# A mixture-of-experts layer whose expert passes 8 to 10 are added back by matmuls instead of by a store and a gather

## The chip, the cores and the metric

One core of one Trainium2 chip runs the whole layer. The metric is the time of one execution on the device, in microseconds (us). Before the change it is 538.73 us, the median of three runs (537.30 to 542.03).

## What is computed

One decoder layer over 512 tokens of width 1024: a projection, four mLSTM heads and eight sliding-window attention heads side by side, an output projection, a layer norm, a two-level mixture of experts (each token picks the best of 4 groups, then the best 2 of the 8 experts in it), and a second layer norm. The change lies in the mixture of experts:

```python
g_idx = jnp.argmax(g_logits, axis=-1)
e_in = jnp.take_along_axis(e_logits, g_idx[:, None, None], axis=1)[:, 0]
top_v, top_i = lax.top_k(e_in, TOP_K_INNER)                      # 2 of 8
top_w = jax.nn.softmax(top_v, axis=-1) * g_p[:, None]
...
for e in range(N_EXPERTS):                                       # 32 experts
    h = jax.nn.silu(xt @ w_exp_gate[e]) * (xt @ w_exp_up[e])     # 1024 -> 256
    out = out + combine[:, e:e + 1] * (h @ w_exp_down[e])        # 256 -> 1024
x = layer_norm(ALPHA * x + out, ln2_w, ln2_b)
```

## The kernel before, in words

The first half of the kernel (projection, heads, first norm, routing) ends at about 269 us and is not touched. What follows are the expert passes.

**Passes.** The 1024 assignments (512 tokens, two experts each) are laid into 13 passes of 128 rows, `ORDER = "BBBABABACBBCC"`. A pass of kind A or B holds two experts, one of kind C four. The six experts of passes 0 to 2 are fixed, the others are ordered by how many tokens chose them, fullest first. Every expert has 3 MB of weights; they stream in through a ring of 16 buffers of 1 MB, in the order of the passes, at most eight transfers at a time. SP's queue issues them, and an issue waits until TensorE has read what the buffer held.

**One pass.** `taken(p)` brings the token rows of two passes, transposed, into `xs`. For most passes it does this by one-hot matmuls (`pairs_x`, 64 matmuls of 128x256; `hots` makes the one-hot tiles `ohr` on VectorE). For the pairs in `GATHER` (4 and 5, 6 and 7) it takes rows that GpSimd's indirect DMA fetched from the copy `xd` of the activations in DRAM (`fetch`, tile `xg`) and turns them by 16 transposes (`pairs_g`). `pass_gu` multiplies by the gate and up weights in four steps; before the last step it turns the hidden rows of the pass before (`dn_t`: two transposes into `ph`, then VectorE copies them to `ht`). `pair_h` makes the hidden rows on ScalarE and VectorE (`hid`). `pass_dn` multiplies the hidden rows of the pass before by the down weights.

**Adding back.** `y_store` scales the result (ScalarE) and GpSimd's queue stores it to the DRAM buffer `yd`. `y_gather` fetches for each chunk of 128 tokens and each of its two experts the row of `yd` (tile `yg`, eight gathers of 512 KB), and VectorE adds it to the sum `x1`. Passes 0 to 10 (`KEPT` = 11) go this way, and `EARLY` puts the eight gathers at the start of pass 11, behind the down product of pass 10. An assignment to pass 11 or 12 reads a row of zeros that the kernel wrote behind the others. Pass 11 goes back by `add_back`: 16 matmuls of 128x512 with a one-hot tile `oh2` (tiles `cb`, two PSUM banks in turn), each pair followed by a VectorE add to `x1`. The rows of pass 12 are handled in the last section.

**Order.** TensorE's order is written out by hand; in the last section (from `p = NP - 1`) that of VectorE, ScalarE and GpSimd too. Every engine executes its own list in order. Tiles `y`, `yg`, `xg`, `xs`, `ohr`, `yh`, `yl`, `oh2` share one pool of 16 buffers ("mix"), so a new tile waits until the last reader of its buffer is done.

## Time and profile before

| | |
|---|---|
| median of 3 runs | 538.73 us |
| the profiled execution | 538.57 us, its span 536.7 us |
| mean granted TensorE clock | 0.929 of full speed |
| TensorE matmul busy | 472.7 us, 88% of the span |
| VectorE, ScalarE, GpSimd busy | 260.8, 163.1, 152.4 us |
| moved by DMA | 139.43 MB, mean 260 GB/s |

The span is the time from the first to the last instruction in the profile; 1.9 us of the execution lie around it. In the rows below L1007 is the matmul of the picks (`pick`), L1062 the transposes of fetched rows, L1094 the gate/up products, L1115 and L1117 the transposes and the copy in `dn_t`, L1125 the down product, L1143 the store to `yd`, L1150 and L1152 the gathers and their adds, L1171 and L1172 the matmuls and adds of `add_back`. The profile counts each gate/up and down matmul twice.

### The profile page before, as it was taken

How to read it: one execution, taken by the hardware profiler on the slowest of the kernel's cores; microseconds unless marked ns; L12 is line 12 of the kernel's file. 1: busy time of each engine (PE TensorE's matmuls, PEld its weight loads, DVE VectorE, ACT ScalarE, POOL GpSimd, SP SyncE). 2: the span in 40 equal slices, each digit the busy share in tenths (PEclk: the TensorE clock that was granted, in tenths of full speed). 3: DMA queues.
4: the chain of work that ended last, by engine and by line, in shares of the span. 5: the costliest groups of instructions: out<-in, count | busy, mean ns of one | idle time of the engine just before them, and what ended most of it. 6: DMA issues, size and time to landing. Idle time of an engine off the chain costs nothing. (4 is left out here: it accounts for less than half of the span.)

```text
span 536.7 us, 8111 instructions
## 1 busy us (share of the span) xinstructions
PE 472.7 (88%) x2904; PEld 315.7 (59%) x2904; DVE 260.8 (49%) x589; ACT 163.1 (30%) x352; POOL 152.4 (28%) x178
## 2 busy tenths in 40 slices
PE   6999899999999999977899999999687996628990
PEld 5999688879899987766735633426112631324420
DVE  3453678884278675688973110303000300144883
ACT  3553545786444322414311111211110111000430
POOL 5479903422120111645821100000000001311451
PEclk9899979999999999999699999999977998757896
DMA  8624212220983539197559999999999999999504
GB/s 231 205 80 122 76 40 78 79 79 8 349 312 96 183 116 280 43 357 255 216 187 394 406 419 406 403 422 395 379 421 422 419 419 422 422 416 423 234 19 159
DMA packets 44907, 139.43 MB, mean 260 GB/s; under 512 B 6386, under 2 KB 17674, under 8 KB 41024
## 3 DMA queue, kind: packets, MB, share of 16 engines
q1 hardware_dynamic: 40944, 126.05, 62.7%
q0 software_dynamic: 3920, 12.84, 6.3%
q8 instruction: 24, 0.39, 0.3%
q14 instruction: 19, 0.16, 0.1%
HBM read 128.68 MB, written 10.49 MB: 259 GB/s over the span
## 5 line engine op out<-in xcount | busy, mean ns | idle before, releaser
L1094 PE MATMUL pg<-we,xs 128*32 128x512 f32 (+1 forms) x608 | 114.0, 645 | 16.1 <-DMA we<-in_w_exp_up 16.1
L1094 PEld LDWEIGHTS pg<-we,xs 128*32 128x32 f32 (+1 forms) x608 | 29.0, 127 | 86.9 <-issue 74.0
L245 PE MATMUL pj<-wh,xh 128*128 128x256 f32 (+1 forms) x224 | 63.8, 287 | 0.6 <-ACT wh L190 0.6
L246 PE MATMUL pj<-wh,xl 128*128 128x256 f32 (+1 forms) x224 | 62.8, 282 | 0.3 <-DVE xl L191 0.3
L1007 PE MATMUL xp<-ohr,x1h 128*128 128x256 f32 (+1 forms) x160 | 45.0, 314 | 18.3 <-ACT xs L1015 8.8
L250 PE MATMUL pj<-wl,xh 128*128 128x256 f32 x192 | 52.5, 279 | 0.0
L1143 POOL DMA_DIRECT2D yd<-y x11 | 6.1, 557 | 158.1 <-ACT y L1142 158.1
L1117 DVE COPY ht<-ph 128x256 f32<-128x256 f32 x13 | 5.5, 423 | 91.9 <-PE ph L1115 91.9
L1125 PE MATMUL yo<-we,ht 128*32 128x512 f32 (+1 forms) x304 | 47.4, 595 | 2.4 <-DVE ht L1117 1.8
L1007 PEld LDWEIGHTS xp<-ohr,x1h 128*128 128x128 f32 x160 | 34.6, 217 | 22.9 <-ACT xs L1015 8.9
L1007 PE MATMUL xp<-ohr,x1l 128*128 128x256 f32 (+1 forms) x160 | 44.1, 309 | 0.0
L245 PEld LDWEIGHTS pj<-wh,xh 128*128 128x128 f32 x224 | 42.4, 189 | 0.9 <-ACT wh L190 0.8
L246 PEld LDWEIGHTS pj<-wh,xl 128*128 128x128 f32 x224 | 42.4, 189 | 0.6 <-DVE xl L191 0.6
L1107 ACT ACTIVATE hid<-pg 128x256 f32<-128x256 f32 x13 | 5.0, 385 | 122.8 <-PE pg L1094 122.8
L250 PEld LDWEIGHTS pj<-wl,xh 128*128 128x128 f32 x192 | 35.6, 188 | 0.0
L1007 PEld LDWEIGHTS xp<-ohr,x1l 128*128 128x128 f32 x160 | 35.0, 219 | 0.0
L191 DVE TENSOR_TENSOR wl<-wraw,wh 128x1024 fp32r<-128x1024 f32 x14 | 21.2, 1528 | 23.0 <-ACT wh L190 22.9
L1125 PEld LDWEIGHTS yo<-we,ht 128*32 128x32 f32 (+1 forms) x304 | 14.4, 119 | 29.2 <-issue 24.4
L190 ACT ACTIVATE wh<-wraw 128x1024 fp32r<-128x1024 f32 (+2 forms) x23 | 23.2, 1021 | 12.3 <-DMA wraw<-in_w_in 3.5
L194 PE MATMUL pj<-xh,wh 128*128 128x512 f32 x64 | 26.7, 417 | 0.0
L196 PE MATMUL pj<-xl,wh 128*128 128x512 f32 x64 | 26.5, 414 | 0.0
L195 PE MATMUL pj<-xh,wl 128*128 128x512 f32 x64 | 26.3, 411 | 0.0
(363 smaller groups left out, 908.2 us busy)
## 6 DMA issues: line engine op xcount, KB each, us to landing
we<-in_w_exp_gate SPq DMA_DIRECT2D x64, 512.0 KB, 11.8
we<-in_w_exp_up SPq DMA_DIRECT2D x64, 512.0 KB, 12.2
we<-in_w_exp_down SPq DMA_DIRECT2D x30, 1024.0 KB, 13.5
wraw<-in_w_in SPq DMA_DIRECT2D x20, 512.0 KB, 3.7
yd<-y POOLq DMA_DIRECT2D x11, 512.0 KB, 7.6
xc<-in_x SPq DMA_DIRECT2D x4, 512.0 KB, 10.0
wo<-in_w_out SPq DMA_DIRECT2D x8, 256.0 KB, 5.0
wo<-in_w_out SPq DMA_DIRECT2D x4, 512.0 KB, 3.6
```

What stands on the lines that cost most here:

```text
L190: A.activation(hi, src, AF.Copy)
L191: eng.tensor_tensor(lo, src, hi, op=OP.subtract)
L194: TE.matmul(o, lh, rh, start=start, stop=False)
L195: TE.matmul(o, ll, rh, start=False, stop=False)
L196: TE.matmul(o, lh, rl, start=False, stop=stop)
L245: TE.matmul(o, xh[j // 2][:, j % 2, cs], ws[i][j][0], start=j == 0, stop=False)
L246: TE.matmul(o, xl[j // 2][:, j % 2, cs], ws[i][j][0], start=False, stop=False)
L250: TE.matmul(o, xh[k // 2][:, k % 2, cs], ws[i][k][1], start=False, stop=k == 7)
L1007: TE.matmul(p_[:, j2, 0:P * n], w[c][:, 2 * g + j2], o[:, c, 0:P * n], start=c == 0 and s == 0 and j2 == 0, stop=c == NCH - 1 and s == 1 a ...
L1094: TE.matmul(pg[s:s + n], xs[k // 4][:, k % 4, P * b + s:P * b + s + n], ws[e][k // 4][:, :, k % 4], start=k == 0, stop=k == 7)
L1125: TE.matmul(py[u][s:s + n], ht[:, j, s:s + n], wt[e][2][j][:, 512 * u:512 * u + 512], start=j == 0, stop=j == 1)
L1143: G.dma_start(yd[p * P:(p + 1) * P], y)
```

## The change

`KEPT` becomes 8 and `GATHER` becomes empty. So:

- all token rows come by one-hot matmuls; the four fetches from `xd` in the loop and their 32 transposes are gone;
- passes 0 to 7 are stored to `yd`, 8 to 10 go back by `add_back`, behind the down product of each, inside passes 9, 10 and 11;
- the eight gathers come in two groups of four: behind the store of pass 7 (in pass 8), and behind the add-back of pass 8 (in pass 9);
- the row of zeros is gone: each `yg` tile is set to zero by GpSimd, and the gather has a bound, so that rows beyond `yd` are left as they are;
- `EARLY` is gone: pass 10's down product stands behind the picks of pass 12 again, as in the other passes.

```diff
-GATHER = (4, 6)
-EARLY = (NP - 2,)
-KEPT = NP - 2
+GATHER = ()
+KEPT = 8
...
-    yd = DR.tile([KEPT * P + 1, DM], F32, name="yd")
+    yd = DR.tile([KEPT * P, DM], F32, name="yd")
...
-    def y_gather():
-        for c in range(NCH):
+    def y_gather(cs):
+        for c in cs:
             for k in range(2):
                 t = slot("yg")[:, :DM]
+                G.memset(t, 0.0)
                 G.indirect_dma_start(out=t, out_offset=None, in_=yd[:, :],
-                                     in_offset=bass.IndirectOffsetOnAxis(ap=yrow[:, 2 * c + k:2 * c + k + 1], axis=0))
+                                     in_offset=bass.IndirectOffsetOnAxis(ap=yrow[:, 2 * c + k:2 * c + k + 1], axis=0),
+                                     bounds_check=KEPT * P - 1, oob_is_err=False)
                 V.tensor_add(x1[c], x1[c], t)
...
-        V.tensor_scalar(yrow, col, float(KEPT * P), None, op0=OP.min)
+        V.tensor_copy(yrow, col)
...
-            early = p in EARLY
-            if early:
-                y_store(pass_dn(dn_t(prev), p - 1), p - 1)
-                y_gather()
             hts = []
-            pg = pg2 if p == 2 else pass_gu(xs, p % 2, p, (lambda: hts.append(dn_t(prev))) if prev and not early else None)
-            if hts:
+            pg = pg2 if p == 2 else pass_gu(xs, p % 2, p, (lambda: hts.append(dn_t(prev))) if prev else None)
+            if prev:
                 ht = hts[0]
...
-            if prev and not early:
-                y_store(pass_dn(ht, p - 1), p - 1)
+            if prev:
+                py = pass_dn(ht, p - 1)
+                if p - 1 < KEPT:
+                    y_store(py, p - 1)
+                else:
+                    y = y_split(py, cws[:, p - 1:p], *y_slots())
+                    add_back(back_hot(slot("oh2", F32R)[:, 0:T], toks(p - 1)), y)
+                if p - KEPT in (0, 1):
+                    y_gather(range(2 * (p - KEPT), 2 * (p - KEPT) + 2))
```

The functions that it now calls in the loop stood in the kernel before and served pass 11 (line numbers of before):

```python
    def y_split(py, cs, yh, yl):                                              # L1131
        for u in range(2):
            us = slice(512 * u, 512 * u + 512)
            A.activation(yh[:, us], py[u], AF.Copy, scale=cs)
            V.scalar_tensor_tensor(yl[:, us], py[u], cs, yh[:, us], op0=OP.mult, op1=OP.subtract)
...
    def add_back(o, y, cs=range(NCH)):
        for c in cs:
            for u in range(2):
                us = slice(512 * u, 512 * u + 512)
                b = bank("cb", tag="pj")
                for i, t in enumerate(y):
                    TE.matmul(b, o[:, c * P:(c + 1) * P], t[:, us], start=i == 0, stop=i == 1)   # L1171
                V.tensor_add(x1[c][:, us], x1[c][:, us], b)                                      # L1172
```

What moves on the engines is shown at three places: VectorE around the gathers, GpSimd's list, and VectorE in the tail. First VectorE's list before, in pass 11 (`ht` and `hid` are those of pass 10's and pass 11's hidden rows, `yg` the gathered rows, `xs` the picked rows for pass 12):

```order
L1117 COPY ht<-ph 128x256
L1152 TENSOR_TENSOR x_2218<-x_2218,yg 128x1024 x2
L1152 TENSOR_TENSOR x_2221<-x_2221,yg 128x1024 x2
L1152 TENSOR_TENSOR x_2224<-x_2224,yg 128x1024 x2
L1152 TENSOR_TENSOR x_2227<-x_2227,yg 128x1024 x2
L1108 TENSOR_TENSOR hid<-hid,pg 128x256
L1013 COPY xs<-xp 128x2x128
```

All eight adds stand together there, ahead of pass 11's hidden rows and of the copy of the picked rows. VectorE's list after the change, from the hidden rows of pass 8 on (the first `ht` below is pass 8's, in the middle of pass 9; the second is pass 9's, in the middle of pass 10):

```order
L1106 TENSOR_TENSOR hid<-hid,pg 128x256
L1152 TENSOR_TENSOR x_2217<-x_2217,yg 128x1024 x2
L1152 TENSOR_TENSOR x_2220<-x_2220,yg 128x1024 x2
L1115 COPY ht<-ph 128x256
...
L1172 TENSOR_TENSOR x_2226<-x_2226,cb 128x512 x2
L1152 TENSOR_TENSOR x_2223<-x_2223,yg 128x1024 x2
L1152 TENSOR_TENSOR x_2226<-x_2226,yg 128x1024
L1115 COPY ht<-ph 128x256
L1152 TENSOR_TENSOR x_2226<-x_2226,yg 128x1024
L1106 TENSOR_TENSOR hid<-hid,pg 128x256
```

Four adds now stand ahead of pass 8's `ht`, and three more, behind the eight adds of pass 8's add-back, ahead of pass 9's `ht`. GpSimd's list after the change from the first store on (before it was a store, two fetches of `xg`, a store, two fetches, nine stores and the eight gathers):

```order
L1141 DMA yd<-y 128x1024 x7
L1148 MEMSET yg 128x1024 x2
L1141 DMA yd<-y 128x1024
L1148 MEMSET yg 128x1024 x2
L1149 DMA yg<-yd,yrow 128x1024 x4
L1148 MEMSET yg 128x1024 x2
L1149 DMA yg<-yd,yrow 128x1024 x2
```

The first four gathers stand behind the eighth store; of the last four the first pair is shown, and the second follows in the same way behind the setting of its tiles. And VectorE's list after the change, in the tail, from the last add of pass 10's add-back to pass 11's `ht` (`ohr` are the one-hot tiles for the rows of pass 12; before, they were made while the picks of pass 12 ran):

```order
L1172 TENSOR_TENSOR x_2226<-x_2226,cb 128x512 x2
L190 TENSOR_TENSOR l2w<-trif,l2w 16x128
L1159 TENSOR_SCALAR oh_4644<-iot,tok_2107 128x256
L1159 TENSOR_SCALAR oh_4644<-iot,tok_2108 128x256
L998 TENSOR_SCALAR ohr<-iot,pcol 128x128
L1000 SCALAR_TENSOR_TENSOR ohr<-iot,pcol,ohr 128x128
...
L1115 COPY ht<-ph 128x256
```

Pass 11's `ht` stands behind the adds of pass 10 and behind eleven small instructions.

## Rows read from the trace of the kernel before

**Rows 1.** The page's part 2: DMA's busy tenths in 40 slices of 13.4 us.

```profile
DMA  8624212220983539197559999999999999999504
```

**Rows 2.** Busy time by stretch: length, PE, PEld, DVE, ACT, POOL, granted clock, DMA share, GB/s.

```profile
405.00:410.00 5.00, 3.10 (x8) 0.77 (x8) 0.00 (x0) 0.00 (x0) 0.00 (x0) 0.54 1.03 421
...
485.00:490.00 5.00, 5.00 (x24) 3.62 (x28) 3.77 (x11) 0.00 (x0) 1.36 (x1) 0.50 1.03 421
490.00:495.00 5.00, 4.48 (x42) 1.34 (x38) 0.42 (x1) 0.00 (x0) 0.00 (x0) 0.93 1.03 423
...
500.00:505.00 5.00, 5.00 (x23) 1.41 (x22) 4.19 (x9) 3.54 (x5) 2.76 (x7) 0.66 0.71 298
```

**Rows 3.** Timeline of TensorE, picks and transposes: start, busy us, line, operation, idle before.

```profile
293.58 0.39 PE L1007 MATMUL xp<-ohr,x1h 128*128 128x256 f32 x1
...
301.08 0.28 PE L1007 MATMUL xp<-ohr,x1l 128*128 128x256 f32 x1
...
315.88 1.16 PE L1062 MATMUL xp<-ident,xg 128*128 128x128 f32 x8
...
318.47 3.65 PE L1125 MATMUL yo<-we,ht 128*64 128x512 f32 x16
```

**Rows 4.** Timeline of TensorE, passes 5, 7, 8 and 10.

```profile
332.96 5.33 PE L1094 MATMUL pg<-we,xs 128*32 128x512 f32 x48
...
340.51 1.16 PE L1062 MATMUL xp<-ident,xg 128*128 128x128 f32 x8
...
357.59 4.47 PE L1094 MATMUL pg<-we,xs 128*32 128x512 f32 x38
...
366.61 0.39 PE L1007 MATMUL xp<-ohr,x1h 128*128 128x256 f32 x1
...
377.97 1.06 PE L1094 MATMUL pg<-we,xs 128*32 128x512 f32 x6
...
397.63 3.62 PE L1125 MATMUL yo<-we,ht 128*32 128x512 f32 x32
...
440.91 3.65 PE L1125 MATMUL yo<-we,ht 128*64 128x512 f32 x16 [0.56 <-ACT y L1142]
```

**Rows 5.** Timeline of TensorE, picks of pass 12 and down product of pass 11.

```profile
474.51 0.48 PE L1007 MATMUL xp<-ohr,x1h 128*128 128x128 f32 x1 [8.79 <-ACT xs L1015]
...
484.73 0.47 PE L1007 MATMUL xp<-ohr,x1h 128*128 128x128 f32 x1 [6.54 <-DVE xs L1013]
...
492.38 3.64 PE L1125 MATMUL yo<-we,ht 128*32 128x512 f32 x32 [0.52 <-DVE ht L1117]
```

**Rows 6.** Timeline of GpSimd: the last store and the first gather.

```profile
445.59 0.53 POOL L1143 DMA_DIRECT2D yd<-y  x1 [4.08 <-ACT y L1142]
454.08 0.98 POOL L1150 DMA_INDIRECT yg<-yd,yrow  x1 [7.97 <-issue]
```

**Rows 7.** Timeline of VectorE, from the first gathered row's add to pass 11's add-back.

```profile
462.72 1.23 DVE L1152 TENSOR_TENSOR x<-x,yg 128x1024 f32<-128x1024 f32 x1 [21.91 <-DMA yg<-yd,yrow]
...
472.70 1.23 DVE L1152 TENSOR_TENSOR x<-x,yg 128x1024 f32<-128x1024 f32 x1 [1.30 <-DMA yg<-yd,yrow]
...
482.78 1.23 DVE L1152 TENSOR_TENSOR x<-x,yg 128x1024 f32<-128x1024 f32 x1 [1.27 <-DMA yg<-yd,yrow]
483.93 0.41 DVE L1108 TENSOR_TENSOR hid<-hid,pg 128x256 f32<-128x256 f32 x1
...
484.59 0.27 DVE L191 TENSOR_TENSOR l2w<-trif,l2w 16x128 fp32r<-16x128 f32 x1
...
488.50 0.42 DVE L1013 COPY xs<-xp 128x256 f32<-128x256 f32 x1
...
497.48 1.36 DVE L1172 TENSOR_TENSOR x<-x,cb 128x512 f32<-128x512 f32 x2
```

**Rows 8.** Groups of instructions on GpSimd: busy us, mean ns of one.

```profile
L389 POOL MEMSET pr<- 128x256 f32 x4 | 1.1, 308 | 0.0
```

**Rows 9.** The DMA issues: count, median us to landing.

```profile
out<-z,row POOLq DMA_INDIRECT x1, 3.3
```

More of the change, by code (lines that the diff above doesn't have):

```diff
@@ L663, in layer_kernel @@
                 need(1)
-    SP.dma_start(yd[KEPT * P:KEPT * P + 1].rearrange("o (k n) -> (o k) n", k=8), warm[0:8])
     identb = C.tile([P, P], BF16, name="identb")
```

## The prediction

> **What bounds the kernel now.** I read the slices first: the DMA engines are full from about 282 us on and empty again at about 503 [rows 1, 2]. This is the weight stream, and one would think that the end is the stream's end. The timelines say otherwise for the last stage. In the picks for pass 12 TensorE stands twice, 8.8 and 6.5 us, for ScalarE's and VectorE's copies of picked rows [rows 5]. VectorE at that time adds gathered rows, one when each gather lands, from 462.72 to 484.0; the hidden rows and the copy that TensorE needs are queued behind the eighth add [rows 7]. From 484.7 TensorE runs on into the down product of pass 11 at 492.38 [rows 5], and from there to the end, 44.3 us later (536.7), stands the tail that the change leaves as it is. The last weights land by about 503 [rows 2]; what needs them is the down product of pass 12, near the end. So the end is set by when the down product of pass 11 can start: now by the gathers, 492.38. I work out that moment for the changed kernel. Before pass 8 the stream does bound: gate/up of pass 8 lasts from 377.97 to 397.63, 19.7 us, where a pass with its weights there takes 7.55 [rows 4].
>
> **Picks for passes 4 to 7.** 64 matmuls take 7.8 us (293.58 to 301.36), the transposes that they replace 2.6 (315.88 to 318.47) [rows 3]. Twice 5.2 makes TensorE 10.4 us later. It is hidden: pass 8 has 12.1 us of waiting (19.7 - 7.55) and pass 7 another 1.5 (357.59 to 366.61 is 9.0) [rows 4], and the stream is ahead, since four fetches of 0.52 MB are gone, 2.1 MB, 5 us at the 421 GB/s of these stretches [rows 2]. Without the cover it would cost the whole 10.4. The down product of pass 7 then ends at 401.25 + 10.4 - 12.1 - 1.5 = **398.0** instead of 401.25. The one-hot tiles cost VectorE work in its idle time, and the stores of passes 8 to 10 go: nothing.
>
> **First four gathers.** From the end of pass 10's down product (444.56) to the first gather, 9.5 us pass: scaling, store, its landing [rows 4, 6]. So the first gather goes at 398.0 + 9.5 = 407.5. Before, the first add came 8.6 us after that, the fourth 18.6, and an add takes 1.23 [rows 6, 7]. The gathers now skip rows: by the reference's routing 617 of the 1024 assignments lie in passes 0 to 7. I scale what is transfer by 0.6: the 10.0 us between first and fourth add to 6.0, and the first 8.6 to 7.3 (one spacing of 3.3 less 40%). The fourth add ends at 407.5 + 7.3 + 6.0 + 1.2 = 422.0, pass 8's `ht` 0.4 later, **422.4**. Bounds: a skipped row may cost as much as a fetched one, 427.8; or each gather lands as fast as the only guarded transfer, 3.3 us [rows 9], and the four adds alone pace it, 416.1. I take the value between, since the guarded transfer met idle DMA engines and these do not. The Trainium skill (DMA: Bandwidth & Descriptors, section Queues, rings and completion order) says that an engine serves the queue rows that have work in turn; two queues would give a gather half the rate. The last four adds, 2.5 us apart for 512 KB [rows 7], agree; the first four, 3.3, do not. By that rule alone the spacing would be 1.5 and everything below 1.5 us earlier.
>
> TensorE has long been there. Its last 48 picks need `ht`'s bank, so they start at 422.4: 5.9 us at full clock. After the 8.8 us wait before, picks ran at a granted clock of 0.50 (1.2 GHz), and it rose about 6 us after TensorE resumed at 484.73 [rows 2, 5]; I add 3.0. They end at 431.3, the down product of pass 8 at 435.0.
>
> **Add-backs of 8, 9, 10.** Pass 11's, in the tail, shows the price: the down product ends at 496.02, the first add starts 1.5 later, and two adds take 1.36 [rows 5, 7]. In the loop two one-hot instructions of 0.3 stand between. So VectorE is done 2.1 + 8 x 0.68 = 7.5 after the down product, TensorE 6.5. For pass 8: TensorE 441.5. Gate/up of pass 10, weights there: 7.55 more, 449.1.
>
> **Last gathers.** Their second pair takes the buffers of pass 8's `yh` and `yl`, free at 441.5. Two tiles are set to zero first. The nearest row is 0.31 us for 256 columns [rows 8]; four times that, 1.2 each (0.3 as lower bound), gives 443.9. First add 7.3 later and 1.2 long, `ht` 0.4: **452.8**, so the down product of pass 9 waits 3.8 us (none by the lower bound, 5.1 by the upper). It ends at 456.5, its add-back at 463.0, gate/up of pass 11 at 470.5, picks (7.8 at most) at 478.3, down product of pass 10 at 482.0, VectorE's adds at 489.5. Behind them VectorE has `l2w`, two one-hot halves and the eight `ohr`, which before took from 484.59 to 488.50, 3.9 [rows 7], while TensorE picked: that cover is gone. `ht` of pass 11 follows, **493.8** against 492.38: +1.4. TensorE waits some 4 us there; the clock may fall again, as it did in pass 9 (0.54, [rows 2]); between 0 and 2.5 us I take 1.0. Weights: pass 12's transfers are released by pass 11's gate/up, 463 to 470, 24 us before the last of them is used. GpSimd's queue has nothing behind the gathers but the tail's small work.
>
> **Sum.** 538.57 + 1.4 + 1.0 = **541.0 us** against this execution's own 538.57; the median of the runs is 538.73, so the two are one number.
>
> **Rivals.**
> *Slower: skipped rows cost as much as fetched ones.* Place: both groups of gathers. The first `ht` comes at 427.8 (+5.4), the second group's first add after 8.6 instead of 7.3 (+1.3): 547.7. It decides from about 3 us on. For it: the indices are 128 in either case, and the issue itself takes GpSimd as long. Against: bytes set the spacing of the last four adds.
> *Faster: gathers land fast.* First `ht` at 416.1 (-6.3), no long wait and so no low clock (-3.0), the second group inside gate/up of pass 10 (-3.8), the last clock loss gone (-1.0): 527; with half of that, 534. I put 530 for it. For it: 315 KB per gather is 0.75 us at 421 GB/s. Against: the DMA share is 1.03 there, weights of passes 9 and 10 are in flight as those of pass 12 were before. The same page of the Trainium skill (section Anatomy of one DMA) gives a GpSimd DMA about 2 us plus its bytes at 436 GB/s, an estimate of 2.7 us for such a gather, and so this rival's time; the trace's 8.6 for 512 KB against 3.2 by that rule speaks against it.
> *Faster by far: the weight stream sets the tail after all.* Stores and fetches take 3.7 MB out, skipped rows 1.7: 12.7 us at 421 GB/s, and the tail starts that much earlier, 526. For it: the full slices. Against: the long waits of TensorE in that stage are for copies, not weights [rows 5], and VectorE's order sets `ht`.
>
> **Chances.** Forecast 0.46, slow gathers 0.27, fast gathers 0.21, stream 0.06. About 1% (5.4 us) is what a measurement of this kernel can tell from no change. Of the fast gathers a fifth stays within it, as does a fifth of the slow ones; of the forecast's own spread a seventh lies above. Faster by over 1%: 0.24; within: 0.48; slower: 0.28. Cases of both signs hold half the chance, so the range reaches from the fast rival's 530 to 550, a little above the slow one's (clock lost at each wait); the forecast's own is 536 to 546.
>
> **What would show it.** TensorE's timeline: the down product of pass 7 ending near 398; one wait of about 8 us inside the picks of pass 10, ended by VectorE's `ht`, then a low clock; a wait of about 4 us ahead of the down product of pass 9; the down product of pass 11 near 494, and 44 us from there to the end. Adds of gathered rows: four ending at about 422, the last near 453. If the first wait is under 3 us, the fast rival holds; if the adds are 3.3 us apart, the slow one. I am wrong in the working if weights, not `ht`, end TensorE's waits after 410, or if the tail itself changes its length.

## The result: slower by about one per cent, and the profile after

The changed kernel takes 545.74 us (median of 20 runs, 541.54 to 552.22), the kernel before, run beside it, 540.36 us (20 runs, 533.67 to 543.78). The ratio is 1.0125, interval [1.0092, 1.0157]; it uses only runs within 1.5% of the fastest of each kernel, so it is not quite the quotient of the two medians (1.0100). Predicted were 541.0, range 530 to 550. The profiled execution after has 546.19 us and a span of 544.5.

TensorE's timeline after the change, from pass 7's down product to pass 11's (start, busy us, line, operation, idle time before and what ended it; L1092 is gate/up, L1123 the down product, L1005 the picks, L1171 the add-back):

```profile
397.76 3.62 PE L1123 MATMUL yo<-we,ht 128*32 128x512 f32 x32
407.18 1.94 PE L1092 MATMUL pg<-we,xs 128*64 128x512 f32 x2 [5.81 <-DMA we<-in_w_exp_up]
410.92 7.54 PE L1092 MATMUL pg<-we,xs 128*64 128x512 f32 x22 [1.80 <-DMA we<-in_w_exp_up]
...
428.14 0.58 PE L1005 MATMUL xp<-ohr,x1h 128*128 128x256 f32 x1 [5.31 <-DVE ht L1115]
435.96 3.64 PE L1123 MATMUL yo<-we,ht 128*32 128x512 f32 x32
441.16 0.47 PE L1171 MATMUL cb<-yh,oh 128*128 128x512 f32 x1 [1.55 <-DVE oh L1159]
...
447.95 5.37 PE L1092 MATMUL pg<-we,xs 128*64 128x512 f32 x24
...
458.35 3.65 PE L1123 MATMUL yo<-we,ht 128*64 128x512 f32 x16 [2.73 <-DVE ht L1115]
...
483.70 3.65 PE L1123 MATMUL yo<-we,ht 128*64 128x512 f32 x16
...
499.87 5.34 PE L1123 MATMUL yo<-we,ht 128*32 128x512 f32 x32 [2.75 <-DVE ht L1115]
```

The three waits that the prediction spoke of are there, each ended by VectorE's `ht`: 5.31 us in the picks of pass 10, 2.73 before pass 9's down product, 2.75 before pass 11's, which starts at 499.87 (492.38 before, [rows 5]). From there to the end are 44.6 us (44.3 before). The 8.8 and 6.5 us waits of before are gone; behind pass 9 no wait for a weight is left.

What stood ahead of these three `ht` on VectorE (L1152 is the add of a gathered row, L1115 the copy to `ht`; before: [rows 7]):

```profile
419.10 1.23 DVE L1152 TENSOR_TENSOR x<-x,yg 128x1024 f32<-128x1024 f32 x1 [20.18 <-DMA yg<-yd,yrow]
422.37 1.23 DVE L1152 TENSOR_TENSOR x<-x,yg 128x1024 f32<-128x1024 f32 x1 [2.04 <-DMA yg<-yd,yrow]
424.64 1.23 DVE L1152 TENSOR_TENSOR x<-x,yg 128x1024 f32<-128x1024 f32 x1 [1.04 <-DMA yg<-yd,yrow]
426.53 1.23 DVE L1152 TENSOR_TENSOR x<-x,yg 128x1024 f32<-128x1024 f32 x1 [0.67 <-DMA yg<-yd,yrow]
427.67 0.42 DVE L1115 COPY ht<-ph 128x256 f32<-128x256 f32 x1
...
456.73 1.23 DVE L1152 TENSOR_TENSOR x<-x,yg 128x1024 f32<-128x1024 f32 x1 [5.52 <-DMA yg<-yd,yrow]
457.88 0.42 DVE L1115 COPY ht<-ph 128x256 f32<-128x256 f32 x1
...
495.49 0.27 DVE L190 TENSOR_TENSOR l2w<-trif,l2w 16x128 fp32r<-16x128 f32 x1
...
499.40 0.42 DVE L1115 COPY ht<-ph 128x256 f32<-128x256 f32 x1
```

GpSimd's part (L1141 the store of pass 7, L1148 the setting to zero, L1149 the gathers; before: [rows 6]):

```profile
402.45 0.53 POOL L1141 DMA_DIRECT2D yd<-y  x1 [10.74 <-ACT y L1140]
402.98 1.86 POOL L1148 MEMSET yg<- 128x1024 f32 x2
410.73 1.12 POOL L1149 DMA_INDIRECT yg<-yd,yrow  x1 [5.89 <-issue]
...
447.86 1.84 POOL L1148 MEMSET yg<- 128x1024 f32 x2 [8.36 <-PE cb L1171]
449.85 1.00 POOL L1149 DMA_INDIRECT yg<-yd,yrow  x1 [0.16 <-POOL yg L1148]
```

From the first gather's issue at 410.73 to the end of the fourth add at 427.76 pass 17.0 us; in the second group the pair issued at 449.85 has its first add at 456.73. And the busy time by stretch (columns as in [rows 2]), where the granted clock, third from the end, shows what the waits cost beside their length:

```profile
425.00:430.00 5.00, 1.86 (x8) 1.86 (x9) 2.75 (x4) 0.00 (x0) 0.00 (x0) 0.56 1.03 421
430.00:435.00 5.00, 5.00 (x35) 5.00 (x34) 2.93 (x8) 0.59 (x1) 0.00 (x0) 0.76 1.03 432
440.00:445.00 5.00, 3.52 (x9) 2.19 (x10) 4.12 (x8) 0.69 (x1) 0.00 (x0) 0.77 1.04 420
...
500.00:505.00 5.00, 5.00 (x32) 1.14 (x28) 0.00 (x0) 0.58 (x1) 0.00 (x0) 0.66 0.22 93
```

After the first of the three waits the clock is below full speed (0.56 and 0.76), and again in pass 8's add-back, behind a wait of 1.55 us (0.77). After the second it stays at 1.00, and after the third it is 0.66. That last one need not be the wait's work: the kernel before has 0.66 in the same 5 us without such a wait [rows 2], and in no_gather and full_rows (below) the same 2.75 us wait is followed by a down product of 3.64 us at full clock. The DMA share is full to 500, but for 0.85 between 470 and 475, and then 0.22: the stream ends at about 501. The slices of the page (as [rows 1], now of 13.6 us) show it full nearly all the way through the passes; a digit of 9 hides shares between 0.9 and 1, and a look at shorter stretches (picks_only, below) finds gaps at the start:

```profile
DMA  8624212221964637368379999999999999998003
```

### The profile page after: what moved, and what is told of

Its sections match the earlier page's. It is cut to its first block, busy times and chain, and to the rows that moved or that the text cites. A ratio compares the mean times of both kernels' runs of the same rounds, so it can differ in the third digit from the quotient of the medians.

```text
span 544.5 us, 8460 instructions
## 1 busy us (share of the span) xinstructions
PE 491.1 (90%) x3048; PEld 336.3 (62%) x3048; DVE 286.5 (53%) x643; ACT 162.6 (30%) x352; POOL 155.7 (29%) x179
## 2 busy tenths in 40 slices
DMA packets 43885, 134.12 MB, mean 246 GB/s; under 512 B 6673, under 2 KB 17953, under 8 KB 40000
## 5 line engine op out<-in xcount | busy, mean ns | idle before, releaser
L1092 PE MATMUL pg<-we,xs 128*32 128x512 f32 (+1 forms) x608 | 102.0, 606 | 8.7 <-DMA we<-in_w_exp_up 8.7
L1092 PEld LDWEIGHTS pg<-we,xs 128*32 128x32 f32 (+1 forms) x608 | 27.7, 121 | 67.6 <-issue 65.5
L1005 PE MATMUL xp<-ohr,x1h 128*128 128x256 f32 (+1 forms) x224 | 59.7, 304 | 7.1 <-DVE ht L1115 5.3
L1005 PE MATMUL xp<-ohr,x1l 128*128 128x256 f32 (+1 forms) x224 | 58.2, 297 | 0.0
L1123 PE MATMUL yo<-we,ht 128*32 128x512 f32 (+1 forms) x304 | 49.2, 620 | 6.5 <-DVE ht L1115 6.5
L1005 PEld LDWEIGHTS xp<-ohr,x1h 128*128 128x128 f32 x224 | 46.6, 208 | 12.9 <-DVE ht L1115 5.5
L1005 PEld LDWEIGHTS xp<-ohr,x1l 128*128 128x128 f32 x224 | 46.5, 208 | 0.0
L1141 POOL DMA_DIRECT2D yd<-y x8 | 4.4, 552 | 124.5 <-ACT y L1140 124.5
L1123 PEld LDWEIGHTS yo<-we,ht 128*32 128x32 f32 (+1 forms) x304 | 14.5, 123 | 35.2 <-issue 25.4
L1115 DVE COPY ht<-ph 128x256 f32<-128x256 f32 x13 | 5.5, 422 | 55.3 <-PE ph L1113 55.3
```

The costliest lines, as they stand in the source:

```text
L1005: TE.matmul(p_[:, j2, 0:P * n], w[c][:, 2 * g + j2], o[:, c, 0:P * n], start=c == 0 and s == 0 and j2 == 0, stop=c == NCH - 1 and s == 1 a ...
L1092: TE.matmul(pg[s:s + n], xs[k // 4][:, k % 4, P * b + s:P * b + s + n], ws[e][k // 4][:, :, k % 4], start=k == 0, stop=k == 7)
L1115: V.tensor_copy(ht, ph)
L1123: TE.matmul(py[u][s:s + n], ht[:, j, s:s + n], wt[e][2][j][:, 512 * u:512 * u + 512], start=j == 0, stop=j == 1)
```

## One clock for all runs

The traces of all kernels differ in when the passes begin: the first gate/up product of pass 0 starts between 264.2 and 270.2 us, also where the code up to there is the same. From that product on they agree far better: in the changed kernel and all nine made from it the down product of pass 6 ends 118.5 us later. So I count from that product. "Stretch" is from it to the end of the span; the ratio is to runs of the kernel before on the same chip. The moments and stretches are differences of rounded figures of one profiled execution each, so their last digit can be off by one.

| kernel | median us | ratio to before, interval | first gate/up | pass 7 down ends | pass 9 gate/up starts | pass 8 down ends | pass 11 down starts | stretch |
|---|---|---|---|---|---|---|---|---|
| before | 540.36 | | 268.2 | 133.0 | 136.4 | 160.7 | 224.2 | 268.5 |
| after | 545.74 | 1.0125 [1.0092, 1.0157] | 269.8 | 131.6 | 137.4 | 169.8 | 230.1 | 274.7 |
| picks_only | 540.88 | 1.0048 [1.0002, 1.0094] | 270.2 | 129.8 | 136.9 | 160.3 | 224.8 | 269.1 |
| no_gather | 531.40 | 0.9889 [0.9806, 0.9972] | 264.3 | 132.0 | 138.0 | 162.4 | 218.5 | 263.1 |
| few_rows | 539.31 | 0.9965 [0.9931, 1.0000] | 268.4 | 131.6 | 137.8 | 165.7 | 224.7 | 271.1 |
| full_rows | 551.45 | 1.0188 [1.0129, 1.0247] | 268.4 | 133.1 | 138.4 | 173.0 | 235.4 | 280.0 |
| adds_late | 545.17 | 1.0136 [1.0079, 1.0193] | 266.6 | 132.2 | 138.1 | 162.7 | 230.2 | 273.1 |
| hots_late | 546.74 | none | 269.1 | 131.7 | 138.2 | 169.6 | 229.3 | 272.2 |
| both_late | 544.56 | 1.0116 [1.0057, 1.0175] | 269.0 | 131.6 | 138.0 | 162.3 | 228.9 | 273.7 |
| pool_adds | 539.35 | 1.0023 [0.9972, 1.0073] | 265.7 | 134.6 | 138.3 | 162.6 | 225.4 | 270.2 |
| pool_both | 535.19 | 0.9943 [0.9899, 0.9987] | 269.1 | 131.7 | 138.2 | 162.8 | 221.3 | 264.3 |
| pool_best | 534.10 | 0.9895 [0.9848, 0.9943] | 269.8 | 134.2 | 138.0 | 162.7 | 219.9 | 262.7 |
| before_pool | 545.05 | 1.0104 [1.0013, 1.0195] | 268.9 | 132.0 | 136.3 | 161.6 | 228.2 | 275.0 |
| before_late | 537.24 | 0.9989 [0.9951, 1.0028] | 264.2 | 133.8 | 136.9 | 161.4 | 225.1 | 270.9 |

Of the 7.8 us between the two spans, 1.6 lie ahead of the passes and are the spread of executions; 6.2 are in the stretch (268.5 to 274.7).

## The experiments

My theory after the result: VectorE's in-order list (the adds of gathered rows, and the small tiles in the tail) holds back `ht` and with it TensorE. The rivals: TensorE's own added work sets the time wherever the adds stand; the weight stream does.

**The gathers left out (no_gather).**

```diff
-                if p - KEPT in (0, 1):
-                    y_gather(range(2 * (p - KEPT), 2 * (p - KEPT) + 2))
```

> From the changed kernel: the eight gathers, the setting of their tiles to zero and their eight adds are left out, so the part of passes 0 to 7 is missing from the sum. My theory: both waits for ht in the loop go as in the run with the adds moved, 9 to 12 us faster than the changed kernel, 534 to 537, and the two runs differ by under 2 us. Rival, the gathers' transfers slow the weight stream: then this run is faster than the one with the adds moved by 3 us or more. Rival, TensorE's own work: 545.7 within 1.5.

The stretch falls from 274.7 to 263.1, that is 11.6 us, and the time to 531.40. TensorE's waits for weights (us in total, count, longest) stay as they were (8.7 in the changed kernel), and of the waits for `ht` the one in the tail remains:

```profile
PE pg L1092 <- DMA we<-in_w_exp_up: 8.9, 3, 6.0
PE yo L1123 <- DVE ht L1115: 2.8, 1, 2.8
```

TensorE's own work is the same here, so that rival falls: the gathers, with their settings to zero and their adds, cost 11.6 us. Without them the changed kernel would be 5.4 us ahead of the kernel before. The time gained is more than the 9 to 12 us expected (14.3 in the medians, 531.40 instead of 534 to 537), and this run's stretch is 10 us shorter than the next one's, where under 2 were expected. That is no sign of slowed weights: TensorE's waits for weights are equal, and the next run failed for another reason.

**The adds moved behind what TensorE needs (adds_late).** `y_due` adds what has been gathered; VectorE's order is as written from pass 9 on.

```diff
-                V.tensor_add(x1[c], x1[c], t)
+                due.append((c, t))
...
+    for ps, engines in ((range(2, KEPT + 1), {ENG.PE}), (range(KEPT + 1, NP - 1), {ENG.PE, ENG.DVE})):
+      with tc.manual_schedule(engines=engines):
+        for p in ps:
...
+            y_due()
             if prev:
                 py = pass_dn(ht, p - 1)
```

> From the changed kernel: the VectorE adds of gathered rows stand behind the hidden rows and the copies of picked rows of the next pass (first four: behind the one-hot tiles for pass 12; last four: behind pass 10's hidden rows) instead of ahead of pass 8's and pass 9's ht. Nothing is left out. My theory (these adds, queued ahead of ht, make TensorE wait): the 5.3 us wait inside the picks of pass 10 and the 2.7 us wait before pass 9's down product go, and with the first the low clock behind it (2.0 us in the picks, up to 1.8 in the add-back of pass 8): 9 to 12 us faster than the changed kernel, 534 to 537. Rival, TensorE's own work (the added add-backs and picks cost their time wherever the adds stand): no change, 545.7 within 1.5. Rival, weight stream: TensorE comes to the weights of passes 10 and 11 earlier and waits for them instead, at most 3 us faster, 543.

Missed: 545.17, a stretch of 273.1. The waits for `ht` went (pass 8's down product ends at 162.7 instead of 169.8), but new ones came, ahead of the add-backs:

```profile
PE cb L1178 <- DVE oh L1166: 12.5, 3, 7.0
```

**The tail's tiles moved behind `ht` (hots_late).**

```diff
-        ob = hots(p, P)
...
         ht = dn_t(prev)
+        ob = hots(p, P)
```

> From the changed kernel: in the last section the one-hot tiles for the rows of pass 12 (eight small VectorE instructions) stand behind pass 11's ht instead of ahead of it. Nothing is left out. My theory: the 2.75 us wait before pass 11's down product goes: 2 to 3 us faster than the changed kernel, 543. Rival, TensorE's own work or the stream: no change, 545.7 within 1.

In the trace the wait before pass 11's down product goes (2.75 to under 0.6) and the stretch is 2.5 us shorter, as expected. The wait is the firmer sign of the two: pass 9's down product took 6.6 us there instead of 3.65 and pass 11's 3.64 instead of 5.34, both by the clock, and that is in the 2.5 too. The four times, 538.20 to 550.47, lie too far apart for a verdict of their own; pool_adds and pool_both below give it.

**Both (both_late).** The two diffs above together.

> Both moves together, nothing left out. My theory: the gains add, 11 to 15 us faster than the changed kernel, 531 to 535, so 5 to 9 us faster than the kernel before. Rival, TensorE's own work: 545.7 within 2. Rival, weight stream: 540 to 543, with waits of TensorE for weights in passes 10 and 11 in the place of those for ht.

Missed: 544.56, a stretch of 273.7. VectorE's timeline shows why (L1106 the hidden rows, L1011 the copies of picked rows, L1158 the adds, L1134 `yl`, L1166 the one-hot tile of the add-back):

```profile
420.44 0.42 DVE L1106 TENSOR_TENSOR hid<-hid,pg 128x256 f32<-128x256 f32 x1 [1.90 <-ACT hid L1105]
423.98 0.69 DVE L1011 COPY xs<-xp 128x512 f32<-128x512 f32 x1 [3.12 <-PE xp L1005]
427.82 0.69 DVE L1011 COPY xs<-xp 128x512 f32<-128x512 f32 x1 [3.15 <-PE xp L1005]
...
431.79 4.87 DVE L1158 TENSOR_TENSOR x<-x,yg 128x1024 f32<-128x1024 f32 x4
436.58 1.41 DVE L1134 SCALAR_TENSOR_TENSOR yl<-yo,cws,yh 128x512 fp32r<-128x512 f32 x2
437.90 0.61 DVE L1166 TENSOR_SCALAR oh<-iot,tok 128x256 fp32r<-128x256 f32 x2
```

The rows had landed, and the four adds ran without a pause, but now between pass 8's down product (it ends at 431.35 there) and what its add-back needs. TensorE stands 7.0 us for them, and 4.0 ahead of pass 9's add-back. So waiting for the rows is not all of it: the adds themselves, 4.9 us for four, make TensorE wait at this place too. It is one place of several. Just before, VectorE stood idle for 1.90, 3.12 and 3.15 us, and the four rows landed there by 418.4, 421.2, 423.2 and 425.5; by these numbers the adds, 1.23 each, would have fitted into the idle stretches one by one. No run tried that order. The next ones take another way, an engine with time to spare.

**The adds on GpSimd (pool_adds).** The gathers come in groups of four, two and two.

```diff
+        ts = []
...
-                V.tensor_add(x1[c], x1[c], t)
+                ts.append((c, t))
+        for c, t in ts:
+            G.tensor_add(x1[c], x1[c], t)
...
-                if p - KEPT in (0, 1):
-                    y_gather(range(2 * (p - KEPT), 2 * (p - KEPT) + 2))
+                if KEPT <= p < KEPT + 3:
+                    y_gather(((0, 1), (2,), (3,))[p - KEPT])
```

> From the changed kernel: the eight adds of gathered rows go from VectorE to GpSimd, and the gathers come in groups of four, two and two (behind pass 7's store, pass 8's and pass 9's add-back). Nothing is left out. Measure in the trace: from the first gate/up product of pass 0 to the end of the span, 274.7 us in the changed kernel, 273.1 with the adds moved later on VectorE, 263.1 without gathers. Theory A (VectorE's in-order list is what the gathers load: 9.8 us of adds and the waits for landing stand ahead of whatever TensorE needs): 263 to 266, and a time of 533 to 537. Theory B (the gathers' landing itself is late, the sum x1 is needed before the rows are there, whichever engine adds): VectorE's adds of pass 8's add-back then wait for GpSimd, and the stretch stays at 271 or more, 542 to 545. Theory C (the gathers' transfers take the weight stream's share): 271 or more, with TensorE waiting for weights in passes 10 and 11.

539.35 us, a stretch of 270.2: 4.5 better in the stretch than the changed kernel, but short of theory A's 263 to 266. Neither B nor C: no wait of VectorE's add-back for GpSimd, none of TensorE for weights behind pass 9. TensorE stood 6.9 us for VectorE ahead of pass 8's add-back.

**And the late tiles of the tail (pool_both).** The diffs of pool_adds and hots_late together.

> The kernel with GpSimd's adds, and also the one-hot tiles for pass 12 behind pass 11's ht. Nothing is left out. Theory A: 2 to 3 us less than the kernel with GpSimd's adds alone, a stretch of 261 to 264, 531 to 535, 1 to 1.5% faster than the kernel before. Theories B and C: 540 or more.

535.19 us, 0.9943 [0.9899, 0.9987] of the kernel before, a stretch of 264.3 (time and stretch are just past the 531 to 535 and 261 to 264 of theory A, far from the 540 of B and C): 4.2 us in the medians and 5.9 in the stretch below pool_adds, of which 2.5 are the tail's tiles (hots_late) and another 2.5 a shorter wait ahead of pass 8's add-back (4.4 us instead of 6.9). What makes this wait shows in VectorE's timeline (L998 are the one-hot tiles for pass 12) beside GpSimd's (L1155 the adds, L1149 the setting to zero), both from this run:

```profile
425.93 2.46 DVE L998 TENSOR_SCALAR ohr<-iot,pcol 128x256 fp32r<-128x256 f32 x1 [0.69 <-POOL x L1155]
428.30 4.24 DVE L998 TENSOR_SCALAR ohr<-iot,pcol 128x256 fp32r<-128x256 f32 x1
```

```profile
423.49 7.13 POOL L1155 TENSOR_TENSOR x<-x,yg 128x1024 f32<-128x1024 f32 x3 [2.72 <-DMA yg<-yd,yrow]
430.56 1.84 POOL L1149 MEMSET yg<- 128x1024 f32 x2
432.56 1.27 POOL L1150 DMA_INDIRECT yg<-yd,yrow  x1 [0.16 <-POOL yg L1149]
```

Two instructions that take 0.60 together in the changed kernel take 6.62 here, from 425.93 to 432.55. GpSimd's three adds follow each other without a pause, 2.4 us each, then two settings. The first instruction starts as the second add does and ends with it (428.38 and 428.23); the second stands through the third add and both settings (to 432.40). The second copy of picked rows and `yl` are queued behind them.

**These tiles made in pass 10 (pool_best).**

```diff
-                if p + 3 < NP:
+                if p + 3 < NP - 1:
                     hn = ready(p + 3)
...
+            if p == NP - 3:
+                hn = ready(NP - 1)
             prev = h
```

> The kernel with GpSimd's adds and the late tiles of the tail, and now also the one-hot tiles for pass 12 made at the end of pass 10 instead of in pass 9. Nothing is left out. In the run before it, two of VectorE's small instructions for these tiles took 6.6 us together instead of 0.6 (425.93 to 432.55) while GpSimd added and set tiles without a pause (423.49 to 432.40), and TensorE then stood 4.4 us for VectorE ahead of pass 8's add-back. Theory A (the two engines shut each other out for such instructions): with GpSimd's adds at the same place the tiles take their 3.2 us undisturbed later, the 4.4 us wait falls to 1 to 2, a stretch of 261 to 262.5 against 264.3, a time of 531 to 533. Rival (the slow pair is a matter of the tiles' buffers, held by gathered rows): the wait moves to pass 10 or 11 and nothing is won, 535.

534.10 us (0.9895 [0.9848, 0.9943] of before), a stretch of 262.7. TensorE's wait for the add-back's tiles, in pool_both and then in this run:

```profile
PE cb L1174 <- DVE oh L1162: 5.5, 2, 4.4
```

```profile
PE cb L1174 <- DVE oh L1162: 3.8, 2, 2.7
```

The longest wait is 2.7 us instead of 4.4, a little more than theory A gave it: the first half of the add-back's own one-hot tile, another instruction of that kind, took 1.83 us there instead of 0.34, beside GpSimd's setting to zero. Nor were the moved tiles undisturbed: they now stand beside GpSimd's next two adds (461.66 to 466.53), where the first four of their eight instructions take 5.7 us instead of about 1.5:

```profile
461.50 2.73 DVE L998 TENSOR_SCALAR ohr<-iot,pcol 128x256 fp32r<-128x256 f32 x2
464.15 3.06 DVE L1000 SCALAR_TENSOR_TENSOR ohr<-iot,pcol,ohr 128x256 fp32r<-128x256 f32 x2
```

TensorE doesn't wait for them there. The time and the stretch miss theory A's 531 to 533 and 261 to 262.5 by little, and the time alone doesn't decide against the rival's 535. The trace does: the wait didn't move to pass 10 or 11, and pass 11's down product starts 1.4 us earlier than in pool_both (219.9 and 221.3), though pass 7 ended 2.5 later. This kernel is faster than the kernel before and the changed one, and its stretch is within a microsecond of that without gathers: theory A stands, with the exclusion of the two engines in it.

**What a skipped row costs: fewer rows, and all rows.**

```diff
-                                     bounds_check=KEPT * P - 1, oob_is_err=False)
+                                     bounds_check=P - 1, oob_is_err=False)
```

> From the changed kernel: the gathers' bound is 127 instead of 1023, so that only rows of pass 0 are fetched and the part of passes 1 to 7 is missing from the sum; indices, issues, tiles and adds are the same. My prediction scaled what is transfer by the share of rows fetched. By bytes: the first add comes under 6 us after the first issue (8.4 in the changed kernel), the adds follow each other by their own 1.23 us, the fourth ends 10 to 11 us after the first issue (17.0), and the time is 6 to 10 us less than the changed kernel, 536 to 540. Rival (a skipped row costs as much as a fetched one, the slower rival of the prediction): 17 us, 545.7 within 1.5.

```diff
-    yd = DR.tile([KEPT * P, DM], F32, name="yd")
+    yd = DR.tile([KEPT * P + 1, DM], F32, name="yd")
...
-                G.memset(t, 0.0)
...
-                                     bounds_check=KEPT * P - 1, oob_is_err=False)
...
-        V.tensor_copy(yrow, col)
+        V.tensor_scalar(yrow, col, float(KEPT * P), None, op0=OP.min)
```

> From the changed kernel: the row of zeros is back and every gather fetches 128 rows, without bound and without setting the tiles to zero. Nothing is left out. By bytes: the fourth add ends 18.5 to 20 us after the first issue (17.0 in the changed kernel, 19.8 in the kernel before); without the 1.9 us of setting tiles to zero ahead of each later pair the second group starts that much earlier: 545 to 549. Rival (a skipped row costs as much as a fetched one): 17 us, and 1 to 2 us faster than the changed kernel, 544.

First and last adds of the first group, with few rows (first issue at 408.94) and then with all (411.11):

```profile
416.37 1.23 DVE L1152 TENSOR_TENSOR x<-x,yg 128x1024 f32<-128x1024 f32 x1 [18.75 <-DMA yg<-yd,yrow]
419.05 3.76 DVE L1152 TENSOR_TENSOR x<-x,yg 128x1024 f32<-128x1024 f32 x3 [1.45 <-DMA yg<-yd,yrow]
```

```profile
419.51 1.23 DVE L1151 TENSOR_TENSOR x<-x,yg 128x1024 f32<-128x1024 f32 x1 [20.45 <-DMA yg<-yd,yrow]
...
428.30 1.23 DVE L1151 TENSOR_TENSOR x<-x,yg 128x1024 f32<-128x1024 f32 x1 [1.26 <-DMA yg<-yd,yrow]
```

| rows fetched in all | first add after first issue | fourth add ends after first issue |
|---|---|---|
| 128 (few_rows) | 7.4 | 13.9 |
| 617 (after) | 8.4 | 17.0 |
| 1024 (full_rows) | 8.4 | 18.4 |
| 1024 (before) | 8.6 | 19.8 |

So skipped rows do save, and the slower rival of the prediction falls: all rows cost 551.45 us, 5.7 more than the changed kernel, a stretch of 280.0. But the saving is small. If each group fetches half of the rows, the first four gathers move 256 KB, 1.26 MB and 2.1 MB in the three runs; from the first to the last that is 1.83 MB in 4.5 us, by this estimate 408 GB/s, about what the full stream moves (421). The two steps by themselves, 3.1 us for 1.0 MB and 1.4 for 0.84, give 320 and 600, so the rate is rough. What is clear is that the time doesn't shrink with the share of rows: even with an eighth of them the first add comes 7.4 us after the first issue. Of few_rows' expectations the time came out (539.31, in 536 to 540) and the steps did not: 13.9 lies between the 10 to 11 of the one and the 17 of the other. full_rows, at 551.45 and 18.4, is outside 545 to 549 and just short of 18.5. The 5.3 us of stretch that all rows cost are more than their 1.4: pass 7 ended 1.5 later in that execution, and pass 9's down product waits 3.7 us instead of 2.7 and then takes 6.3 instead of 3.65, at a lower clock; pass 11's, at full clock there, gives 1.7 back.

**The picks alone (picks_only).** From the kernel before:

```diff
-GATHER = (4, 6)
+GATHER = ()
```

> From the kernel before: only the first part of the change, the token rows of passes 4 to 7 come by one-hot matmuls and are not fetched. Nothing is left out. My prediction's step (10.4 us more of TensorE work, hidden by the waits for weights in passes 7 and 8): no change against the kernel before, stretch 268.5 within 1.5. Rival, the cover is gone since the weight stream is released later: stretch 270 to 279. Rival, the stream gets the 5 us head start of the missing fetches: stretch 264 to 266.

540.88 us, ratio 1.0048 [1.0002, 1.0094], a stretch of 269.1 against 268.5: nearly nothing, as expected. Pass 7's down product ends 3.2 us earlier (129.8 instead of 133.0), which is just what the prediction's step said (398.0 instead of 401.25). What it didn't say is that TensorE then waits for pass 9's weights, which come no earlier than before (136.9 and 136.4), so that these 3.2 us are lost again. The stream kept nothing of the missing fetches: for a time it stood still for buffers. First what SP's queue waited for TensorE's down product up to 420 us (total, count, longest), in the kernel before and in this run, then a 10 us stretch of each:

```profile
SPq L597 <- PE yo L1125: 6.5, 2, 6.0
```

```profile
SPq L597 <- PE yo L1125: 21.1, 5, 9.4
```

```profile
298.20:308.20 10.00, 10.00 (x59) 5.17 (x58) 0.83 (x2) 1.76 (x3) 1.56 (x2) 1.00 1.03 404
```

```profile
300.20:310.20 10.00, 10.00 (x61) 5.05 (x63) 3.35 (x10) 1.79 (x4) 0.55 (x1) 1.00 0.86 324
```

The longer picks make TensorE release weights later, and the transfers that wait for those buffers start later. Between 10 and 130 us of the stretch DMA moves 48.4 MB in the kernel before and 46.1 here, less by about the four fetches; the weight queue's part is 42.5 and 42.3, the same.

**The kernel before with GpSimd's adds (before_pool).**

```diff
+        ts = []
...
-                V.tensor_add(x1[c], x1[c], t)
+                ts.append((c, t))
+                if len(ts) > 4:
+                    c_, t = ts.pop(0)
+                    G.tensor_add(x1[c_], x1[c_], t)
+        for c, t in ts:
+            G.tensor_add(x1[c], x1[c], t)
```

> From the kernel before: the eight adds of gathered rows go from VectorE to GpSimd, the gathers otherwise as they were. Nothing is left out. Theory A (the adds in VectorE's list make the 8.8 and 6.5 us waits in the picks of pass 12): these waits go, at most 15 us less, bounded by the weights of pass 12; a stretch of 254 to 260 against 268.5 in the kernel before, 525 to 532. Theory B (landing): TensorE goes through the picks and stands later, in pass 11's add-back, for the rows: 4 us less or none, 536 to 540. Theory C (stream): TensorE stands for pass 12's weights instead, 536 to 540.

Missed: 545.05 us, slower. ScalarE's timeline, first in the kernel before, then here (L1015 copies picked rows to `xs`):

```profile
474.09 0.37 ACT L1015 COPY xs<-xp 128x256 f32<-128x256 f32 x1 [11.66 <-DVE x L1152]
```

```profile
477.50 0.37 ACT L1015 COPY xs<-xp 128x256 f32<-128x256 f32 x1 [13.61 <-POOL x L1156]
```

ScalarE adds nothing; it waits until an add has released a buffer for the picked rows. So no buffer of the pool's 16 is free for it at that time, and gathered rows hold some of them. A slower adder holds them longer (2.4 us for an add on GpSimd instead of 1.23). ScalarE's long wait in the kernel before was for a buffer, not for VectorE's turn.

**The picked rows given their buffers first (before_late).** From the kernel before:

```diff
             if early:
                 y_store(pass_dn(dn_t(prev), p - 1), p - 1)
-                y_gather()
...
                 xs = taken(p + 1, hn)
...
+            if early:
+                y_gather()
```

> From the kernel before: in pass 11 the eight gathers are written behind the picks for pass 12 instead of ahead of them, so that the picked rows get their buffers first and VectorE copies them ahead of most adds of gathered rows. Nothing is left out. Theory A (buffers and VectorE's order make the 8.8 and 6.5 us waits in these picks: in the trace of before ScalarE's copy waited 11.7 us for an add of gathered rows to give its buffer free): both waits go, then TensorE comes to pass 12's weights about 15 us earlier than they can be there; they were in by 503, 12.6 MB at 420 GB/s, so that the first third is there at about 483 and the down product of pass 11 starts at 480 to 486 instead of 492: 527 to 533, and the kernel that stores all passes is then level with the best form of the changed one, 534.1. Rival (the gathers, with fewer free buffers and behind the picks, land later, and pass 11's add-back waits for them): TensorE's wait moves to the add-back, 536 to 542.

Both waits in the picks are gone, as expected, and still theory A missed: 537.24 us, where the kernel before beside it took 539.49, a ratio of 0.9989 [0.9951, 1.0028]. The rival's time (536 to 542) came out, but not its reason, for TensorE doesn't wait in the add-back. It now waits for the weights of pass 12, in the gate/up part ahead of pass 11's down product (two of four such rows, 12.2 us in all):

```profile
474.46 1.89 PE L1094 MATMUL pg<-we,xs 128*32 128x512 f32 x2 [7.48 <-DMA we<-in_w_exp_up]
479.44 1.92 PE L1094 MATMUL pg<-we,xs 128*32 128x512 f32 x2 [3.09 <-DMA we<-in_w_exp_up]
```

Its down product of pass 11 starts at 225.1 of the stretch, in the kernel before at 224.2. So the waits for copies in the kernel before were covered: behind them the weights came just in time. My 480 to 486 for that moment was 489.2, in an execution whose passes began 4.0 us earlier; on the clock of the kernel before that is 493.3.

## Why the number held, and where its account did not

The number: 541.0 predicted, 545.74 measured, inside the range and just inside the forecast's own 536 to 546. The change itself was put too small, 2.4 us instead of 5.4 in the medians (6.2 in the stretch). So the result lies between two of my classes: 1.25% slower, interval from 0.9 to 1.6, is nearer to "slower by over 1%" (0.28) than to "within 1%" (0.48). Step by step (1.6 us of each delay are the later start of the passes in the execution after):

| moment | predicted | measured | late by |
|---|---|---|---|
| pass 7's down product ends | 398.0 | 401.4 | 3.4 |
| first gather issued | 407.5 | 410.7 | 3.2 |
| fourth add ends | 422.0 | 427.8 | 5.8 |
| pass 8's down product ends | 435.0 | 439.6 | 4.6 |
| TensorE done with pass 8's add-back | 441.5 | 448.0 | 6.5 |
| pass 9's down product ends | 456.5 | 462.0 | 5.5 |
| pass 10's down product ends | 482.0 | 487.3 | 5.3 |
| pass 11's `ht` done | 493.8 | 499.8 | 6.0 |

- *What bounds the kernel now: wrong.* The prediction said that the gathers, not the stream, set the start of pass 11's down product, since the long waits are for copies. before_late takes these waits away, and pass 11's down product starts no earlier. I had looked only at the last weights, which the down product of pass 12 needs near the end; but the first quarter of pass 12's gate/up stands ahead of pass 11's down product, and its weights were as late as the rows. A wait names only the one that came last. The "stream" rival, put at 0.06, described the kernel before; its consequence is that the waits removed were worth next to nothing by themselves, and that what could be won comes from the 5.3 MB less that the change moves (139.43 to 134.12). SP issues the last weight transfer at 224.9 of the stretch in the kernel before, at 218.9 in the changed one and at 218.0 in pool_best. pool_best, with the same bytes as the changed kernel, starts pass 11's down product at 219.9 instead of 224.2; no_gather, which moves still less (131.58 MB), at 218.5. Neither waits for pass 12's weights.
- *The reason for the first wait: half wrong.* "Queued behind the eighth add" holds for VectorE's copy. ScalarE's copy, 8.8 us, waited for a buffer (before_pool).
- *Picks hidden: right; the stream's head start: it lasted to pass 7 and no further.* From the first gate/up product the predicted end of pass 7 is at 129.8 (398.0 - 268.2), and picks_only has 129.8. The changed kernel has 131.6, and the kernels made from it, alike up to pass 6, have 131.6 to 134.6; what makes them differ is open. Fewer bytes don't advance a stream that waits for buffers: pass 9's weights came no earlier.
- *The gathers: mechanism right, size off.* Store to first gather 9.35 us, predicted 9.5. Issue to fourth add 17.0, predicted 14.5: I took 5.3 us off the 19.8 of the kernel before, by scaling both the landing and the spacing by the share of rows. The runs fit bytes at the stream's rate better: 0.4 of 2.1 MB at 421 GB/s are 2.0 us, which gives 17.8. The slow rival (19.8) and the fast one (8.2) were further off. Of the two rules of the Trainium skill cited there (DMA: Bandwidth & Descriptors, sections Anatomy of one DMA and Queues, rings and completion order) neither does better: a landing of 2.7 us is far under the 6.4 us and more that the first gather of a group took in every run, and with half the rate for gathers the 1.83 MB would by estimate have taken 8.7 us, not 4.5.
- *The clock: right after the first wait, too small in all.* The picks of pass 10 took 7.9 us (8.9 predicted), but the clock fell again in pass 8's add-back (0.77; 8.3 us on TensorE instead of 6.5) and in pass 11's down product (0.66; 5.34 instead of 3.64). I had 1.0 for all of that. A wait of that size doesn't settle it: after 2.73 us ahead of pass 9's down product the clock stayed full in the changed kernel (3.65 us) and fell in hots_late (2.92 us, then 6.6).
- *The later waits: right.* 2.73 us ahead of pass 9's down product (3.8 predicted), 2.75 ahead of pass 11's (about 4), a tail of 44.6 (1.7 of it the slower down product). hots_late, and pool_both against pool_adds, confirm the small tiles as the cause of the last.

So the sum's mechanism, VectorE's list ahead of `ht`, is what the runs show (no_gather, 11.6 us; and hots_late to pool_both, where the adds on GpSimd, with the gathers in other groups, take 7.9 us off the stretch), with two qualifications: adds_late and both_late show that it is the adds' own time as well as the landing, and the one later place tried on VectorE won nothing back; the adds spread over its idle stretches are untested. I had no rival in which the change is worth 5 us and its gathers and adds take twice that away. That no wait for weights was left behind pass 9 in the changed kernel was in part luck: I had set the stream aside because the waits in the kernel before were for copies, and they say nothing about the weights.

## What to carry to other kernels

A wait names only what came last: before counting its removal as a gain, ask when the next input was there, best by taking the wait away in a run. Moving work later in an engine's list only moves the wait if it lands where that list has no idle time: look for the idle stretches first, or give it to another engine, and then check what both engines shut each other out of, and who holds the buffers meanwhile. And fewer bytes help a stream only while it is short of bandwidth, not of buffers.

## What the runs showed of the hardware that was not expected

- VectorE's small instructions with SBUF on both sides stood still while GpSimd worked without a pause: two 128x256 TENSOR_SCALARs took 6.62 us in pool_both and 6.60 in pool_adds instead of 0.60; one took 1.83 us in pool_best instead of 0.34, and there two SCALAR_TENSOR_TENSORs took 3.06 instead of 0.88. Copies out of PSUM beside GpSimd's adds kept their 0.69 us (pool_both at 424.55). The Trainium skill (SBUF — State Buffer, section SBUF: two separate sides) describes an exclusive lock of a port pair that VectorE and GpSimd share, which whoever starts first keeps for the whole instruction. The traces agree with such a lock; the waiting side didn't always get in at the next change of instruction, for the first of pool_both's two waited out one GpSimd instruction (2.46 us) and the second three (4.24 us).
- Under a full weight stream the first GpSimd gather of a group landed 7.3 us after its issue with an eighth of the rows (few_rows), 8.3 with 60% (after) and 8.3 to 10.0 with all (full_rows, before, picks_only); in the second group of few_rows it was 6.4. The guarded transfer of the kernel before, with DMA nearly idle, took 3.3 [rows 9].
- Executions differ by up to 6 us in when the passes begin (264.2 to 270.2), and then, in the changed kernel and the nine made from it, agree within 0.1 us for 118 us. A difference of a few us between single executions says little; the stretch says more.
